# State-space stage of a decoder trunk: the rotated drive is added on TensorE, with new tables, tap layout and order

## Chip, cores and metric

The kernel runs on one core of one Trainium2 chip. The metric is the device time of an execution in microseconds; each measurement is the median of several executions. The profile is of one further execution.

## The reference, cut to what matters

A trunk of two layers on 512 tokens of 1024 channels, all in f32. The first layer is a diagonal state-space mixer with a gated output and a squared-ReLU MLP; then come shared keys and values, an attention layer with forget gates and a second MLP. The change lies in the state-space mixer alone:

```python
lam_bar = jnp.exp(lam * dt)                       # 64 groups x 64 complex states
b_bar = ((lam_bar - 1.0) / lam)[..., None] * b
bu = jnp.einsum('blgc,gpc->blgp', uf, b_bar)      # 16 channels of a group drive 64 states
_, states = lax.associative_scan(_ssm_binop, (a_elems, bu), axis=1)   # s[t] = lam_bar*s[t-1] + bu[t]
y = jnp.real(jnp.einsum('blgp,gcp->blgc', states, c))
y = y + d_skip.reshape(N_GROUPS, SSM_GROUP) * uf
z = jax.nn.gelu(y.reshape(bsz, length, D_MODEL))
zw = z @ w_glu
return zw[..., :D_MODEL] * jax.nn.sigmoid(zw[..., D_MODEL:])
```

## The kernel before

The 64 groups are worked in eight blocks `b` of 8 groups. The 512 tokens are cut into 64 chunks of T = 8. Real and imaginary parts of the 64 states fill the 128 partitions. Within a chunk the answer is a causal filter with eight taps of 16 x 16 (a Toeplitz matrix per group); between chunks the state runs through a scan. A step of the scan multiplies by a complex number; the kernel splits this into its size (r8, in the scan) and its angle, which is undone before the scan and put back behind it, by tables of cosine and sine per group and chunk. For one block these are the steps; the names are those of `ORDER`:

- `win1, win2, wina` build the input matrix Win: two DVE products of 1024 elements, and an accumulating transfer of POOL's queue that adds tB to Win (512 KB). `wo1, wo2, woa` do the same for the output matrix, the first half of the tile TW.
- `pw, wt`: eight TensorE transposes of Win and two ACT copies. `pd` (`c_pd`): the drive, eight matmuls from WinT and the transposed inputs Uall into a bank of PSUM.
- `tab0, tab3`: the tables CS. DVE adds a coarse and a fine angle, and six ACT passes (four absolute values, two sines, L368 to L373) make cosine and sine.
- `cos, ds, da`: the drive times cosine into cc, the drive times minus sine into dt, both on DVE, and two accumulating transfers that add dt to cc with the partition halves swapped (`add_swapped`, L345).
- `dec, scan`: the decays, and the scan over cc into tz (L647). `P1, P2, padd`: the states times cosine and sine, again two products and two swapped additions by transfer. `py2`: states times output matrix.
- `pt, ks, kd, kw, tr`: the taps. Eight matmuls with 16 columns of weights (the last step of Win), each of 128 columns of Wout, go to partitions r to r+16 of two banks; two ACT copies put them into `ks`, DVE adds the skip term at lag 0, one transfer of SP's queue writes them to a DRAM buffer (`KD`, two of them), and `tr`, also on SP's queue, reads them back as a Toeplitz matrix into the second half of TW. `py1` multiplies the inputs with it. py1 and py2 add up in one bank; each alternates between the left and the right 64 columns of the array.
- `gelu, zt, zh, lo`: GELU on ACT, four transposes, a rounded copy by ACT and the remainder by DVE, both written with a stride so that tokens come in order.
- `gl, gs, gv, gp`: the first weights of the gated output (GLU): load, rounding, remainder, and matmul pieces that need only the first four blocks of Z. GLU accumulators hold two banks of PSUM for each of the groups 0, 1 and 2.

The order of the stage is written out by hand: each word of `ORDER` issues the instructions of a step to their engines, which run them in that order, each waiting for its operands. Apart from that, buffers set waits. Win has three, tB and P two, TW four (two of each kind A and B, handed out by the string `WQ`), PSUM eight banks. Behind the stage comes the rest of GLU (L810), where TensorE is busy throughout.

## Time and profile before

| | us |
|---|---|
| median of 3 runs | 1204.86 (1197.44 to 1206.99) |
| profiled execution, its own time | 1199.35 |
| its span | 1197.6 |
| mean granted TensorE clock over the span | 0.972 |

The span is what the profiler saw from the first to the last instruction; the execution's own time holds 1.75 us more. In the rows, L12 is line 12 of the kernel, PE is TensorE's matmuls, DVE VectorE, ACT ScalarE, POOL GpSimd and SP the engine whose queue issues most transfers. `x32` counts instructions; an f32 matmul is two of them. An idle time stands in brackets with what ended it.

### The profile page before, as it was taken

Reading aid. Unit: us, or ns where it says so; the run is one execution under the profiler, and the core shown is the slowest. Engines: PE = TensorE matmul, PEld = TensorE weight load, DVE = VectorE, ACT = ScalarE, POOL = GpSimd, SP = SyncE. Lnnn points to the kernel's source line nnn. Section 1 sums busy time; section 2 is a strip of 40 time slices with the busy share of each in tenths; the row PEclk is TensorE's granted clock in tenths of the full one; section 3 lists DMA queues with packets and bytes.
Section 4 is the critical chain, followed back from the end, with each engine's and each line's share of the span. In section 5 each row is a group of like instructions: output and inputs, shape, how many; then the busy total and the mean of one; then the engine's idle time right before and its main releaser. Section 6 shows DMA issues by size and latency. Waiting matters only on the chain.

```text
span 1197.6 us, 19030 instructions
## 1 busy us (share of the span) xinstructions
PE 1119.2 (93%) x7189; PEld 996.8 (83%) x7189; DVE 912.1 (76%) x1639; ACT 607.8 (51%) x1106; POOL 291.2 (24%) x298
## 2 busy tenths in 40 slices
PE   1678899999999999999999999888899999999997
PEld 1567688899999898998888999776899898999986
DVE  8976548799877778768566878875999777778754
ACT  4985355454434444336345666554755444343433
POOL 4234214422121212203102222314322312213101
PEclk9878899999999999999999999989899999999999
DMA  7997753143322323233244444311143323233222
GB/s 165 218 183 151 176 165 106 42 143 99 122 90 90 107 86 124 88 103 117 65 132 133 107 107 133 98 54 53 35 128 104 111 82 124 88 117 96 89 88 71
DMA packets 109388, 131.37 MB, mean 110 GB/s; under 512 B 9360, under 2 KB 87984, under 8 KB 109296
## 3 DMA queue, kind: packets, MB, share of 16 engines
q1 hardware_dynamic: 104432, 117.57, 32.9%
q0 software_dynamic: 4864, 12.59, 6.1%
q8 instruction: 57, 0.93, 0.3%
q14 instruction: 35, 0.29, 0.1%
HBM read 103.21 MB, written 2.74 MB: 88 GB/s over the span
## 4 chain that ended last, share of the span: by engine, by line
PE 79%; DVE 8%; DMA 5%; ACT 3%; issue 3%; SPq 0%; POOL 0%; DVEq 0%; ACTq 0%; POOLq 0%
PE pu L919 25%; PE po L810 16%; PE pvs L1484 14%; PE pk L810 6%; PE pv L810 6%; PE pvs L1130 2%; PE po L1268 2%; DMA cc<-dt 1%; PE ptp L1234 1%; PE pf L1118 1%; DMA TW<-tB 1%; DVE prob L1229 1%; DMA bc<-in_ssm_b_im_dram 1%; DMA TW<-kd 1%; PE pv L731 1%
## 5 line engine op out<-in xcount | busy, mean ns | idle before, releaser
L919 PE MATMUL pu<-hm,ar 128*128 128x256 f32 x1536 | 228.9, 284 | 3.2 <-ACT hm L863 2.2
L919 PEld LDWEIGHTS pu<-hm,ar 128*128 128x128 f32 x1536 | 204.4, 193 | 4.5 <-ACT hm L863 2.6
L810 PE MATMUL po<-at,wt 128*128 128x512 f32 x768 | 176.9, 389 | 0.0
L1484 PE MATMUL pvs<-wt,at 128*128 128x512 f32 (+1 forms) x768 | 175.5, 388 | 0.0
L898 POOL TENSOR_TENSOR ar<-ar,st 128x256 f32<-128x256 f32 x62 | 71.8, 1160 | 423.1 <-DVE ar L894 404.3
L124 ACT ACTIVATE wt<-st 128x1024 fp32r<-128x1024 f32 x110 | 116.2, 1057 | 114.0 <-PE po L810 30.3
L810 PEld LDWEIGHTS po<-at,wt 128*128 128x128 f32 x768 | 143.2, 188 | 29.1
L1484 PEld LDWEIGHTS pvs<-wt,at 128*128 128x128 f32 x768 | 142.6, 188 | 28.8
L128 DVE TENSOR_TENSOR wt<-st,wt 128x1024 fp32r<-128x1024 f32 x90 | 117.1, 1302 | 27.9 <-ACT wt L124 27.7
L919 PE MATMUL pu<-hd,x 128*128 128x256 f32 x768 | 136.3, 285 | 0.0
L887 ACT ACTIVATE ar<-ar 128x512 fp32r<-128x512 f32 x128 | 77.0, 627 | 89.9 <-PE pu L919 83.7
L919 PEld LDWEIGHTS pu<-hd,x 128*128 128x128 f32 x768 | 113.4, 193 | 2.9 <-issue 0.5
L888 DVE TENSOR_TENSOR ar<-ar 128x512 fp32r<-128x512 f32 x128 | 88.8, 700 | 31.0 <-ACT ar L887 31.0
L887 ACT ACTIVATE x<-st 128x512 fp32r<-128x512 f32 x62 | 36.3, 625 | 99.8 <-PE pvs L1484 48.9
L128 POOL TENSOR_TENSOR wt<-st,wt 128x1024 fp32r<-128x1024 f32 x20 | 48.2, 2408 | 143.6 <-ACT wt L124 125.5
L894 DVE TENSOR_TENSOR ar<-st 128x512 f32<-128x512 f32 x62 | 50.6, 819 | 32.8 <-DMA st<-in_mlp_w_dram 32.1
L810 PE MATMUL pv<-zt,wt 128*128 128x512 f32 x312 | 72.4, 391 | 0.2 <-ACT hT L992 0.2
L810 PEld LDWEIGHTS pv<-zt,wt 128*128 128x128 f32 x312 | 58.2, 188 | 12.3 <-ACT hT L992 0.4
L1220 ACT ACTIVATE prob<-psx,mx 128x128 f32<-128x128 f32 (+1 forms) x64 | 33.8, 528 | 60.2 <-DVE mx L1218 60.2
L899 POOL TENSOR_TENSOR ar<-ar,st 128x256 f32<-128x256 f32 x62 | 60.4, 977 | 4.2
L1039 ACT ACTIVATE at<-c 128x512 fp32r<-128x512 f32 x64 | 39.7, 630 | 39.3 <-DVE c L1037 39.1
L1025 DVE TENSOR_TENSOR hT<-hT,po 128x512 f32<-128x512 f32 x64 | 43.4, 679 | 16.8 <-PE po L810 16.8
(333 smaller groups left out, 2046.2 us busy)
## 6 DMA issues: line engine op xcount, KB each, us to landing
st<-in_mlp_w_dram SPq DMA_DIRECT2D x126, 512.0 KB
st<-in_ssm_w_glu_dram SPq DMA_DIRECT2D x16, 512.0 KB
st<-in_w_kvf_dram SPq DMA_DIRECT2D x14, 512.0 KB
hx<-kt SPq DMA_DIRECT2D x48, 128.0 KB
Win<-tB POOLq DMA_DIRECT2D x8, 512.0 KB, 7.3
TW<-tB POOLq DMA_DIRECT2D x8, 512.0 KB, 6.3
TW<-kd SPq DMA_DIRECT2D x8, 512.0 KB
st<-in_attn_wq_dram SPq DMA_DIRECT2D x8, 512.0 KB
```

Of the source, the lines that this page charges most:

```text
L124: S.activation(wt[:, 0], st, AF.Copy)
L128: (G if slot[1] == "A" and CFG["x"][7 + lows[0] % 3] == "G" else V).tensor_tensor(wt[:, 1], st, wt[:, 0].bitcast(F32), op=ALU.subtract)
L810: TE.matmul(pts[m], wt[:, a, k, m * P:(m + 1) * P], acts[k0 + k][:, b], start=(first and k0 == parts[0][0] and k == 0 and n == 0), stop=(k ...
L887: S.activation(X[0], src, AF.Copy)
L888: V.tensor_tensor(X[1], src, X[0].bitcast(F32), op=ALU.subtract)
L894: V.tensor_tensor(Ta[:, :, js].rearrange("p w j n -> p j w n"), f[:, :, 1:3], f[:, :, 0:1].broadcast_to([P, 2, 2, P]), op=ALU.add)
L898: e.tensor_tensor(Tb[:, 0, js], Ta[:, 0, js], v[:, :, 1, 0], op=ALU.add)
L899: e.tensor_tensor(Tb[:, 1, js], Tb[:, 0, js], v[:, :, 1, 1], op=ALU.add)
L919: TE.matmul(self.acc[p], self.W[p][:, a, j], self.H.moving(p, j, b), start=(p == g[0] and j == 0 and n == 0), stop=(p == g[-1] and j == 3 ...
L1025: V.tensor_tensor(hT[:, m, :], hT[:, m, :], po[j], op=ALU.add)
L1039: S.activation(at_[:, 0], c, AF.Square)
L1484: TE.matmul(po[:, cols], A[k][:, b], wts[k // 2][:, a, k % 2, cols], start=start and n == 0, stop=stop and n == 3 * len(ks) - 1)
```

## The change

- The drive. One DVE instruction `(CS - 1) * drive` makes both rotated parts at once (`c_cd`, 1024 elements). `da` is now two TensorE matmuls into one bank, the first part times the identity, the second times a signed swap of the partition halves (`swp`); the scan reads that bank. The states get the same single instruction (`c_pp`); their addition `padd` stays a transfer.
- The tables. `tab0` makes two angles (the second shifted by a quarter turn, whose rounding is added to `tk` and `ta`), and `tab3` is a sine and a square with factor, 2 sin^2, which is one minus the cosine of the double angle.
- The taps. `pt` takes 32 columns of weights (the last two steps of Win, of which the last counts), goes round four column groups of the array, and fills a quarter of one bank per group; `ks` is one copy over 128 partitions; `kd` adds on 128 partitions; `kw` is four transfers per block with runs of 128 bytes; there are four DRAM buffers. The skip term's tile and mask are laid out accordingly (`dl`, `dg`), and the zeros of the DRAM buffers come from a small tile.
- The last transposes write their bank with a stride of four, so that `zh` and `lo` read and write contiguously.
- The gain of the first two blocks moves from POOL to DVE. Six memsets of constants go or change.
- `ORDER` and `WQ` are new. Among other things: blocks 0 and 1 are begun together, the rest of the group factors (`LR`, `mR`) stands behind their products, the transposes of the inputs (`u`) stand ahead of the first `pw`, tables 0 and 4 ahead of `wt_0`, and pieces of GLU groups 0 and 1 ahead of block 5.

```diff
@@ -33,25 +33,24 @@
-WQ = "AABBABABAB"
+WQ = "BAABBABBAB"
 ORDER = """
...
+tk dl_0 gR gl_0 rxv gnl decS_0 win2V_1 sw_2_0 xsS_0_0 sw_2_1 win2V_0 xsS_1_0 gl_1 win1V_0 gl_2 kz win1V_1
+wina_0 xsS_1_1 gn wo1V_0 wina_1 dl_1 xsS_0_1 wo2V_1 u_6 sw_0_1 u_3 wo1V_1 u_2 u_1 usS_2 taV woa_1 u_4 usS_1
+tab0V_0 u_0 usS_4 u_5 usS_0 tab0V_4 u_7 tab3_0 tab0V_1 tab3_4 wo2V_0 pw_0 tab0V_2 woa_0 wtS_0 LR tab3_2 pd_0
+mR usS_7 pw_1 usS_3 dg usS_5 win2V_2 wtS_1 win1V_2 gs_1 pd_1 win2V_3 usS_6 wina_2 tab3_1 wo2V_2 pt_1 wo1V_2
...
+py2_4 cd_7 pw_6 gelu_4 wo1V_7 zt_4 woa_7 wtS_6 da_7 tr_5 pd_6 scan_7 decS_6 pp_7 pt_6 cd_6 padd_7 zt_3 ksS_6
+kd_6 zhS_3 da_6 kw_6 lo_3 zhS_4 lo_4 pt_7 scan_6 gp_1_3 ksS_7 kd_7 kw_7 gp_0_3 gp_1_2 tr_6 py1_5 tr_7 py2_5
+gp_0_2 pp_6 gs_2 gelu_5 gv_2 padd_6 py1_6 gp_2_0 py1_7 py2_7 gp_2_1 gelu_7 py2_6 zt_5 gp_2_3 zhS_5 gelu_6 lo_5
...
@@ -193,6 +187,10 @@
             dup = sp.tile([P, 64], F32, name="dup")
             G.tensor_copy(dup[0:64], ident[0:64, 0:64])
             G.tensor_copy(dup[64:128], ident[64:128, 64:128])
+            swp = sp.tile([P, P], F32, name="swp")
+            G.memset(swp, 0.0)
+            G.tensor_scalar(swp[0:64, 64:128], ident[0:64, 0:64], -1.0, None, ALU.mult)
+            G.tensor_scalar(swp[64:128, 0:64], ident[64:128, 64:128], -1.0, None, ALU.mult)
             pa = pst("pa")
             for h in range(2):
...
@@ -243,16 +241,16 @@
             mask = sp.tile([P, GC], F32, name="mask")
             for q in range(4):
-                G.tensor_copy(mask[q * 32:q * 32 + 32], ident[q * 32:q * 32 + 32, q * 32:q * 32 + GC])
-            ks = sp.tile([P, T, GB, GC], F32, name="ks")
-            G.memset(ks, 0.0)
-            KD = [dp.tile([GC, 2 * T - 1, P], F32, name=f"kd{i}", tag=f"kd{i}", bufs=1) for i in range(2)]
+                G.tensor_copy(mask[q * 32:q * 32 + 32], ident[q * 32:q * 32 + 32, q * 32 + GC:q * 32 + 2 * GC])
+            zk = sp.tile([GC, P], F32, name="zk")
+            G.memset(zk, 0.0)
+            KD = [dp.tile([GC, 2 * T - 1, P], F32, name=f"kd{i}", tag=f"kd{i}", bufs=1) for i in range(4)]
             def dl(i):
-                for h in range(2):
-                    v = (ssm_d, mix_norm)[i][0][h * 512:h * 512 + 1]
-                    DMA.dma_start(dgb[i][:, h * GB:h * GB + GB].rearrange("p g c -> p (g c)"),
-                                  bass.AP(tensor=v.tensor, offset=v.offset, ap=[[P, 4], [0, 32], [1, P]]))
+                v = (ssm_d, mix_norm)[i][0][0:1]
+                for q in range(4):
+                    DMA.dma_start(dgb[i][q * 32:q * 32 + 32],
+                                  bass.AP(tensor=v.tensor, offset=v.offset + q * 32, ap=[[0, 32], [P, NB], [1, 32]]))
             def gnl():
                 for i, gsrc in enumerate((mlp_norm[0], kv_norm, mix_norm[1], mlp_norm[1])):
...
@@ -359,18 +357,15 @@
             def tab0(q, e=G):
                 gs = slice(q * GB, (q + 1) * GB)
                 CS[q] = ap_.tile([P, 2, GB, NCH], F32, name="cs", tag="act")
-                e.tensor_tensor(CS[q][:, 1].rearrange("p g (a b) -> p g a b", a=T),
-                                tA[1][:, gs, :].unsqueeze(3).broadcast_to([P, GB, T, T]),
-                                tA[0][:, gs, :].unsqueeze(2).broadcast_to([P, GB, T, T]), op=ALU.add)
+                for i in range(2):
+                    e.tensor_tensor(CS[q][:, i].rearrange("p g (a b) -> p g a b", a=T),
+                                    tA[1][:, gs, :].unsqueeze(3).broadcast_to([P, GB, T, T]),
+                                    tB_[:, i, gs, :].unsqueeze(2).broadcast_to([P, GB, T, T]), op=ALU.add)
             def tab3(q):
-                co, si = fl(CS[q][:, 0]), fl(CS[q][:, 1])
-                S.activation(co, si, AF.Abs)
-                S.activation(si, si, AF.Abs, bias=sg[:, 9:10])
-                S.activation(co, co, AF.Abs, bias=sg[:, 8:9])
-                S.activation(si, si, AF.Abs, bias=sg[:, 8:9])
-                S.activation(co, co, AF.Sin, scale=TWO_PI, bias=sg[:, 4:5])
-                S.activation(si, si, AF.Sin, scale=sg[:, 6:7], bias=sg[:, 7:8])
+                t = CS[q].rearrange("p i g j -> p (i g j)")
+                S.activation(t, t, AF.Sin, scale=3.1415925)
+                S.activation(t, t, AF.Square, scale=math.sqrt(2.0))
             ss = sp.tile([P, T], F32, name="ss")
             junk = bp.tile([P, 512], F32, name="junk", tag="P3", bufs=1)
...
@@ -453,6 +448,12 @@
                     V.tensor_scalar(tks[i], tA[i], MAGIC, MAGIC, ALU.add, ALU.subtract)
                     yield
                 V.tensor_tensor(tA[1], tA[1], tks[1], op=ALU.subtract)
+                yield
+                V.tensor_tensor(tA[0], tA[0], tks[0], op=ALU.subtract)
+                yield
+                V.tensor_scalar(tB_[:, 1], tA[0], sg[:, 7:8], None, ALU.add)
+                yield
+                V.tensor_scalar(tks[1], tB_[:, 1], MAGIC, MAGIC, ALU.add, ALU.subtract)
             GA, GR = slice(0, 2 * GB), slice(2 * GB, NG)
...
@@ -585,31 +586,32 @@
                     cpy(e, WT[b][:, hf * 4:hf * 4 + 4, :], PW[b][hf].rearrange("p (g c) -> p g c", g=4))
             def b_pt(b):
-                TP[b] = [pst("pt") for _ in range(2)]
-                r = b % 4 * 32
-                for g in range(GB):
-                    TE.matmul(TP[b][g // 4][r:r + GC, (g % 4) * P:(g % 4 + 1) * P], W["Win", b][:, g, T - 1],
-                              W["Wout", b][:, g], start=True, stop=True)
+                TP[b] = pst("pt")
+                for gh in range(2):
+                    for q in range(4):
+                        TE.matmul(TP[b][q * 32:q * 32 + 32, gh * P:(gh + 1) * P],
+                                  W["Win", b][:, 2 * q + gh, T - 2:T].rearrange("p t c -> p (t c)"),
+                                  W["Wout", b][:, 2 * q + gh], start=True, stop=True)
+
+            KS = {}
             def b_ks(b, e=S):
-                r = b % 4 * 32
-                for hf in range(2):
-                    cpy(e, ks[r:r + GC, :, hf * 4:hf * 4 + 4].rearrange("p l g c -> p g l c"),
-                        TP[b][hf][r:r + GC].rearrange("p (g l c) -> p g l c", g=4, c=GC))
+                KS[b] = bp.tile([P, T, 2, GC], F32, name="ks", tag="ks", bufs=2)
+                cpy(e, KS[b].rearrange("p l g c -> p g l c"),
+                    TP[b][:, 0:2 * P].rearrange("p (g l c) -> p g l c", g=2, c=GC))
             def b_kd(b):
-                r = b % 4 * 32
-                d = ks[r:r + GC, 0]
-                V.tensor_tensor(d, d, dgb[0][r:r + GC, b // 4 * GB:(b // 4 + 1) * GB], op=ALU.add)
+                d = KS[b][:, 0]
+                V.tensor_tensor(d, d, dgb[0][:, b].rearrange("p (g c) -> p g c", c=GC), op=ALU.add)
             def b_kw(b):
-                r = b % 4 * 32
-                DMA.dma_start(KD[b % 2][:, T - 1:2 * T - 1].rearrange("c l n -> c (l n)"),
-                              ks[r:r + GC].rearrange("p l g c -> p (l g c)"))
+                for q in range(4):
+                    DMA.dma_start(KD[b % 4][:, T - 1:2 * T - 1, q * 32:q * 32 + 32],
+                                  KS[b][q * 32 + GC:q * 32 + 2 * GC].rearrange("p l g c -> p l (g c)"))
             def b_tr(b):
                 Toep = W["TW", b][:, 1].rearrange("p g t c -> p (g t c)")
-                v = KD[b % 2][0:1, 0:1, 0:1]
+                v = KD[b % 4][0:1, 0:1, 0:1]
                 DMA.dma_start(Toep, bass.AP(tensor=v.tensor, offset=v.offset,
                                             ap=[[P, T], [(2 * T - 1) * P, GC], [1, T * P]]))
                 TP[b] = Toep.rearrange("p (t g c) -> p g t c", g=GB, c=GC)
...
@@ -628,34 +630,39 @@
                               start=True, stop=True)
                 DD[b] = PD[b].rearrange("p (g j) -> p g j", g=GB)
-            def c_cos(b):
-                CC[b] = g2("cc", 2)
-                V.tensor_tensor(CC[b], DD[b], CS[b][:, 0], op=ALU.mult)
-
-            def c_ds(b):
-                DS[b] = g2("dt")
-                V.scalar_tensor_tensor(fl(DS[b]), PD[b], -1.0, fl(CS[b][:, 1]), op0=ALU.mult, op1=ALU.mult)
+            def rot(o, b, v):
+                V.scalar_tensor_tensor(o, CS[b], 1.0, v.unsqueeze(1).broadcast_to([P, 2, GB, NCH]),
+                                       op0=ALU.subtract, op1=ALU.mult)
+
+            def c_cd(b):
+                CC[b] = bp.tile([P, 2, GB, NCH], F32, name="cc", tag="cc", bufs=1)
+                rot(CC[b], b, DD[b])
+
+            DA = {}
+
+            def turn(name, a):
+                pd = pst(name)
+                for i, m in enumerate((ident, swp)):
+                    TE.matmul(pd, m, fl(a[:, i]), start=i == 0, stop=i == 1)
+                return pd
             def c_da(b):
-                add_swapped(fl(CC[b]), fl(DS[b]))
+                DA[b] = turn("da", CC[b])
             TZ = {}
             def c_scan(b):
                 tz = bp.tile([P, GB * NCH + 1], F32, name="tz", tag="tz", bufs=1)
                 V.memset(tz[:, 0:1], 0.0)
-                V.tensor_tensor_scan(tz[:, 1:GB * NCH + 1], fl(CC[b]), fl(DEC[b]), 0.0, op0=ALU.add, op1=ALU.mult)
-                PP[b] = [g2("P1", 2), g2("P2", 2)]
+                V.tensor_tensor_scan(tz[:, 1:GB * NCH + 1], DA[b], fl(DEC[b]), 0.0, op0=ALU.add, op1=ALU.mult)
                 TZ[b] = tz[:, 0:GB * NCH].rearrange("p (g j) -> p g j", g=GB)
-            def c_p2(b, e=V):
-                e.tensor_tensor(PP[b][1], TZ[b], CS[b][:, 1], op=ALU.mult)
-
-            def c_p1(b, e=V):
-                e.tensor_tensor(PP[b][0], TZ[b], CS[b][:, 0], op=ALU.mult)
+            def c_pp(b):
+                PP[b] = bp.tile([P, 2, GB, NCH], F32, name="PP", tag="PP", bufs=2)
+                rot(PP[b], b, TZ[b])
             def c_padd(b):
-                add_swapped(fl(PP[b][0]), fl(PP[b][1]))
+                add_swapped(fl(PP[b][:, 0]), fl(PP[b][:, 1]))
             def py(b, w, u, start, stop):
                 for g in range(GB):
...
@@ -680,25 +687,21 @@
             def e_zt(b):
                 ZP[b] = pst("zt")
+                zv = ZP[b].rearrange("p (j h t) -> p h j t", h=2, t=4)
                 for t in range(4):
-                    TE.transpose(ZP[b][:, t * P:(t + 1) * P], YU[b][:, t].rearrange("p g c -> p (g c)"), ident)
-
-            def zview(b, i):
-                return Z[b][:, i].rearrange("p (j h t) -> p h t j", h=2, t=4)
-
-            def zsrc(b):
-                return ZP[b].rearrange("p (t h j) -> p h t j", h=2, t=4)
+                    TE.transpose(zv[:, :, :, t], YU[b][:, t].rearrange("p g c -> p (g c)"), ident)
             def e_zh(b, e=S):
                 Z.append(act_t("zt"))
-                cpy(e, zview(b, 0), zsrc(b))
+                cpy(e, Z[b][:, 0], ZP[b])
             def e_lo(b):
-                V.tensor_tensor(zview(b, 1), zsrc(b), zview(b, 0).bitcast(F32), op=ALU.subtract)
+                V.tensor_tensor(Z[b][:, 1], ZP[b], Z[b][:, 0].bitcast(F32), op=ALU.subtract)
             def dg():
                 V.tensor_tensor(dgb[0], dgb[0], dgb[1], op=ALU.mult)
-                V.tensor_tensor(dgb[0], dgb[0], mask.unsqueeze(1).broadcast_to([P, 2 * GB, GC]), op=ALU.mult)
+                d = dgb[0].rearrange("p b (g c) -> p (b g) c", c=GC)
+                V.tensor_tensor(d, d, mask.unsqueeze(1).broadcast_to([P, 2 * NB, GC]), op=ALU.mult)
             def gn():
                 pg = pst("pg")
```

## Rows read from the trace of the kernel before

**Rows 1.** The page's first line: span of the profiled execution
```profile
span 1197.6 us, 19030 instructions
```

**Rows 2.** Windows: PE, PEld, DVE, ACT, POOL busy, clock, DMA share, GB/s
```profile
40.00:60.00 20.00, 13.58 (x89) 11.69 (x85) 19.44 (x24) 19.26 (x33) 8.24 (x11) 0.80 1.01 204
60.00:80.00 20.00, 13.87 (x150) 11.71 (x148) 17.34 (x23) 17.61 (x28) 7.96 (x12) 0.84 1.03 189
80.00:100.00 20.00, 15.27 (x194) 14.18 (x194) 11.80 (x18) 17.08 (x29) 7.96 (x11) 0.76 0.85 169
100.00:120.00 20.00, 20.00 (x225) 17.50 (x224) 12.49 (x18) 8.81 (x13) 7.54 (x12) 0.83 0.75 144
120.00:140.00 20.00, 15.70 (x152) 12.90 (x151) 10.93 (x17) 7.74 (x10) 6.22 (x10) 0.85 0.82 167
```

**Rows 3.** TensorE's timeline: start, us, instructions, [idle before, releaser]
```profile
43.64 1.91 PE L591 MATMUL pt<-TW,Win 128*16 128x128 f32 x16 [1.17 <-DMA TW<-tB]
...
81.50 1.97 PE L663 MATMUL py<-TW,Uall 128*64 128x64 f32 x32 [5.43 <-ACT ks L353]
...
132.16 1.15 PE L663 MATMUL py<-TW,P 128*64 128x64 f32 x32 [1.94 <-DMA P<-P]
134.79 1.98 PE L663 MATMUL py<-TW,Uall 128*64 128x64 f32 x32 [1.48 <-DMA TW<-kd]
...
150.29 1.65 PE L731 MATMUL pv<-zt,wt 128*128 128x512 f32 x6
```

**Rows 4.** Chain of waits, first 230 us: start, us, what
```profile
49.05 5.83 DMA cc<-dt
...
75.69 10.97 DMA cc<-dt
```

**Rows 5.** Instructions by form, 40 to 160: busy, mean ns, idle before
```profile
L697 DVE TENSOR_TENSOR zt<-zt 128x512 fp32r<-128x512 f32 x8 | 9.2, 1146 | 7.8 <-ACT zt L353 7.6
L353 ACT ACTIVATE zt<-zt 128x512 fp32r<-128x512 f32 x8 | 9.0, 1131 | 13.1 <-PE zt L684 13.0
...
L353 ACT ACTIVATE ks<-pt 16x512 f32<-16x512 f32 x16 | 8.9, 581 | 7.2 <-PE pt L591 7.1
...
L531 DVE TENSOR_TENSOR Win<-ML,XY 128x1024 f32<-128x1024 f32 x7 | 8.5, 1217 | 3.7 <-PE pt L591 3.7
...
L373 ACT ACTIVATE cs<-cs,sg 128x512 f32<-128x512 f32 x8 | 6.4, 798 | 0.0
...
L637 DVE SCALAR_TENSOR_TENSOR dt<-pd,cs 128x512 f32<-128x512 f32 x8 | 5.5, 689 | 8.6 <-DMA cc<-dt 8.5
...
L368 ACT ACTIVATE cs<-cs 128x512 f32<-128x512 f32 x8 | 5.0, 627 | 0.0
```

**Rows 6.** TensorE's timeline, the f32 matmul pb of the last MLP
```profile
873.11 1.02 PE L975 MATMUL pb<-dg,ones 128*128 128x512 f32 x2
873.56 0.92 PE L919 MATMUL pu<-hd,x 128*128 128x256 f32 x3
```

**Rows 7.** DMA queues, 0 to 172, then 18 to 26: packets, MB, share
```profile
q0 software_dynamic: 4864, 12.59, 42.4%
...
DMA packets 1831, 0.65 MB, mean 82 GB/s; under 512 B 1638, under 2 KB 1798, under 8 KB 1831
...
q1 hardware_dynamic: 1831, 0.65, 45.9%
```

**Rows 8.** Timeline, 20 to 45 us, DVE and TensorE
```profile
21.43 1.01 DVE L467 TENSOR_TENSOR LL<-tmp 128x384 f32<-128x384 f32 x2
...
25.18 1.21 DVE L536 TENSOR_TENSOR tB<-ML,XY 128x1024 f32<-128x1024 f32 x1
...
40.47 2.00 PE L627 MATMUL pd<-Uall,WinT 128*128 128x64 f32 x16
```

**Rows 9.** SP's queue: tap copies (min/median/max), the TW load's wait
```profile
L607 SPq DMA_DIRECT2D kd<-ks x8: 302/308/330, 48.4 to 128.2; - x8
...
SPq L613 <- DMA kd<-ks: 27.5, 6, 7.4
```

More of the change, by code (lines that the diff above doesn't have):

```diff
@@ L283, in body @@
             f8, f64 = small("f8"), small("f64")
-            tA = [sp.tile([P, NG, T], F32, name=f"tA{i}") for i in range(2)]
-            tks = [bp.tile([P, NG, T], F32, name="tk", tag="P2", bufs=2) for i in range(2)]
+            tB_ = sp.tile([P, 2, NG, T], F32, name="tAB")
+            tA = [tB_[:, 0], sp.tile([P, NG, T], F32, name="tA1")]
+            tks = [bp.tile([P, 2, NG, T], F32, name="tk", tag="PP", bufs=2)[:, 0] for i in range(2)]
             def angles():
```

51 lines of the change are left out of this document (18 added, 33 removed).

## Prediction

> **What bounds the kernel now.** Read the split of the execution first: the profiled one is 1199.35 us, its span 1197.6 [rows 1], and the three timed runs have a median of 1204.86 (1197.44 to 1206.99). One per cent, 12 us, is about what a measurement of this kernel can tell from no change. Everything that the change touches lies in the first 160 us, the state-space stage; what follows is matmul after matmul, so a microsecond gained here should be a microsecond gained at the end.
>
> Then read the stage in pieces of 20 us [rows 2]. From 40 to 140 us TensorE is busy 78.4 us of 100, so idle for 21.6. The granted clock lies between 0.76 and 0.85, a mix of stretches at 1.2 and at 2.4 GHz; busy time times what is missing of the clock (13.58 x 0.20 and four more) gives 14.4 us lost to it. So 36 us of TensorE's time could at most come back. In the same rows three other columns are nearly full: DVE 19.4 and 17.3 of 20 up to 80 us, ACT 19.3, 17.6 and 17.1 up to 100 us, the DMA engines 1.01 and 1.03 up to 80 us and 0.75 to 0.85 later. No single engine bounds the stage: it is a relay with little slack in the front and a queue of TensorE work at the back.
>
> Third, what ended TensorE's pauses [rows 3]. There are nine in this stretch. Three end with ACT (5.43 us the longest) and make 9.8 us; three end with the accumulating transfers into Win and TW (1.17 the first), 5.1 us; two with the accumulating transfer P (1.94 the second), 5.2 us; one, 1.48, with the round trip of the taps through DRAM. The chain of waits names a fourth kind that makes no TensorE pause of its own but holds DVE: cc<-dt, 5.83 and 10.97 us for two additions of the rotated drive [rows 4].
>
> **The change part by part.** *Drive added by TensorE.* Gone per block: two DVE products (0.69 us each) [rows 5] and two accumulating POOL transfers of 128 KB, whose 16 issues leave POOL's queue to Win, TW and P. New: one DVE instruction of 1024 elements, which I price at the 1.22 us of a 1024-element product [rows 5], since at 512 elements this form (0.689) costs what a product does; and two f32 matmuls of 512 columns. One such matmul is two instructions, and in the one place where before has it the second starts 0.45 us after the first [rows 6]: 0.9 us, so 1.8 us per block and 14.4 us for eight at 2.4 GHz, twice that at 1.2. The scan then reads PSUM; no row of the stage prices that, and I take no difference, since the drive's product dt reads PSUM at the price of any other 512-element product (its bounds: nothing, and the 0.53 us by which 1.22 exceeds 0.69).
> The new wait is that of da on its DVE product, in TensorE's own queue. Behind da_1 and da_0 stand the transposes and drive of block 2, behind da_7 and da_6 the drive of block 6 and the taps of block 7. The producer takes 1.22 us once DVE comes to it, and DVE's order puts it right after work that TensorE needs anyway. I count no pause for it beyond those that I leave standing below; in the middle, a DVE that is late by two of its 1024-element products would cost 2.4 us for each such da.
> Banks of PSUM come out even, as the taps take one instead of two and the added drive one; but the pieces of GLU group 1 now start before block 5, so GLU holds four of eight banks from there, where before it held two. Its cover is that a block's banks turn over while GLU pieces run.
>
> *Taps in four column groups.* Before, eight matmuls per block with 16 columns of weights take 1.91 us [rows 3], 0.119 per instruction of 128 columns. After, the same eight go to four column strips of the array. The nearest row is py, which alternates between two strips: 32 instructions of 64 columns in 1.15 us, 0.036 each, where half of 0.119 would be 0.060: a factor of 1.7 for two strips. Twice that factor once more gives 0.119 / 2.8 = 0.042, 0.7 us per block; the ends are 1.91 (no overlap) and 0.48 (four at once). I take 0.6 to 0.7 and a saving of 1.25 x 8 = 10 us. The Trainium skill, TensorEngine Tiling (Array Packing), Theoretical Speedup, allows up to four times for 32 columns or fewer, which would make the saving 11.4; Key Properties in it says that changing the tiling mode drains the engine, which before pays as well, with its 16-column weights.
> TensorE's net is thus +4 us at full clock; at the stage's mean clock, 0.82, it is +5.
>
> *Tables by sine squared.* Six ACT passes of 512 elements per block, 0.63 to 0.80 us [rows 5], 4.3 in all, become two of 1024; twice a single pass bounds each between 1.25 and 1.6, and overlapped issue takes some off: 2.5 per block, 1.8 less. DVE makes both angles: one more product, +0.69. The new order puts tables between gelus three times, so two more table loads.
> *Last transposes interleaved.* The strided copy and its remainder (1.13 ACT, 1.15 DVE) [rows 5] become contiguous, 0.6 and 0.69: half a microsecond less on each. The transposes now write strided; no row prices that, and I take nothing (its bounds are minus nothing and 0.6 us per block, doubling them).
> *Taps' copy.* Two ACT copies of 0.58 [rows 5] become one over 128 partitions, about 0.5. Together ACT loses some 2.9 us per block, 23 in the stage, and DVE stays even (-0.15, +0.69, -0.46 and little else). So the three pauses that ACT ends should go: **+9.8**.
>
> *What the DMA engines get back and pay.* The software queue takes 42.4% of 172 us for 12.59 MB [rows 7]: 5.8 us of all 16 engines per MB. The 2.1 MB of the drive free 12 us. But the taps go to DRAM in pieces of 128 bytes: 512 per block, 4096 in all. The nearest row is the stretch with 1638 packets under 512 bytes of 1831: 45.9% of 8 us x 16 engines / 1831 = 32 ns each [rows 7], so 4096 x 32 / 16 = 8 us. The net is 4 us of relief, and the drive's six microseconds of landing leave the path. I let half of the 10.3 us of pauses at accumulating transfers go: **+5**.
> The Trainium skill, DMA: Bandwidth & Descriptors, Specifications, says that under 512 bytes the engine reads, modifies and writes. Were each small piece then twice as dear, an estimate by that page, the 8 would be 16 us and the relief a loss of 4; the mechanism is a rival below.
>
> *Clock.* One and the same product py stands at 1.98 us right behind two pauses and at 1.15 elsewhere [rows 3]: the two levels of the clock. Fewer pauses should leave fewer stretches at the lower one. I take half of 14.4: **+7**.
>
> *Order and queues.* On DVE the reduction of angles, the gains and the row norms now stand ahead of the first Win products. Before, the rest of the group factors took DVE from 21.43 to 25.18, then came win2 and win1 of block 0 [rows 8]; the norms followed. After, these 3.75 us are postponed, and ahead of the end of win1_0 come the norms (sixteen tiny instructions, some 2.4), the angles and gains (seven instructions of 512 elements or so, by 0.4 to 0.69 each an estimate of 3.9) and win2 of block 1 (1.14 as issued): 2.4 + 3.9 + 1.14 - 3.75 = 3.7 us later. A part is covered, since the transposes of U, which before followed pw_0, run in that time; the first drive product, pd_0 at 40.47 [rows 8], I put **2 us** later (between 0 and 3.7).
> SP issues four tap transfers per block where it issued one of 0.31 us [rows 9]; the TW load behind them on SP already waits 4.6 us each time (27.5 over 6). Three more issues at 0.31 to 0.6 add 0.9 to 1.8 us, and what is queued behind on SP, the TW load of the block and the next GLU weights, waits as long. With four DRAM buffers instead of two the copies no longer wait for the load before last. For the middle blocks other work hides it. For the last block it does not: after its taps come the copy, the scan ahead and kd (2), four issues (2), the landing (4.6), then issue and landing of TW (4 to 5, an estimate below the 5.83 us of an accumulating transfer [rows 4]), some 13 us. Queued on TensorE against it are four GLU pieces (1.65 each [rows 3]), and both products of block 5: 9 us. So **4 us** stay exposed, where before lost 1.48.
>
> Sum: 9.8 + 5 + 7 = 22 recovered; 5 + 2 + 4 = 11 paid. **11 us faster**: 1188.4 for an execution like the profiled one, which was 5.5 below the median, so 1194 (1204.86 - 11) for the median, with 1188 to 1200 for this case alone.
>
> **Rivals.** *The relay closes up*: the drive's detour of six microseconds was what kept later blocks from starting, and GLU pieces, ready earlier, fill what is left. Then all pauses but the 1.48 go and 12 of 14.4 us of clock; the costs shrink to 4 + 2 + 2. 32 - 8 = 24: 1181. For it speaks that cc stands in the chain with 10.97 us for one block; against it the full DVE up to 80 us.
> *DMA stays the bound*: the small packets eat the relief, and accumulating transfers end the same pauses. 9.8 + 4 of clock - 11 = 3: 1202. For it speaks a share of 1.01 to 1.03.
> *The strips do not overlap*: the taps stay at 1.91 and 10 / 0.82 = 12 us of the sum fall away: 1206. Against it speaks py.
> *SP becomes the bound, slower than before*: the TW load waits on SP for its four tap transfers, and the next block's stand behind it. At 2.4 of issue, 9 of landing and 0.6 for the load, eight blocks take 96 us. From 52, the first copy's 48.4 [rows 9] plus the late start, that is 148 for the last load, where before issued it about eight after 128.2. Twelve later, with the 2 us of the order, less what ACT gives back in the tail, 13 in all: 1218. It decides from a landing of about 8 us; at 4.6 it is harmless.
>
> **How the numbers follow.** Forecast 0.40, closed relay 0.28, DMA bound 0.14, strips 0.08, SP 0.10. Faster by over 1% means under 1192.8: the closed relay and the lower third of the forecast, 0.40. Slower by over 1% is most of the SP case and a little of the strips, 0.10. The rest, 0.50, is within 1%. The range leaves out the lowest of the closed relay and the SP case: 1179 to 1210.
>
> **What would show it.** ACT's share between 40 and 100 falls from nine tenths to about six; pt takes 0.6 to 0.7 us per block; da takes 1.8 us at full clock, 3.6 at half; pauses ended by ACT vanish; the last GLU piece of the stage ends some 11 us earlier. I am wrong if DMA waits take those pauses over, if the granted clock stays at 0.82, or if py1 of the last blocks waits over 4 us for TW.

## The result, and the profile after

The changed kernel takes 1214.67 us (median of 4, 1213.57 to 1221.75), the kernel before, measured beside it, 1204.69. The ratio is 1.010 with a 95% interval of 1.006 to 1.014: slower by 10 us, where 11 us faster was forecast. The profiled execution took 1215.23 us, 15.9 more than the one of before (1199.35). That one lies 5 us under its kernel's median, so differences between these two traces are larger than between the medians. The span, to set beside [rows 1]:

```profile
span 1213.5 us, 19061 instructions
```

Windows of the kernel after, 40 to 140 us, with the columns of [rows 2]:

```profile
40.00:60.00 20.00, 12.82 (x79) 11.11 (x78) 14.54 (x21) 12.19 (x18) 2.58 (x3) 0.77 0.59 114
60.00:80.00 20.00, 17.24 (x189) 12.49 (x189) 18.53 (x23) 6.55 (x10) 5.26 (x8) 0.89 0.85 161
80.00:100.00 20.00, 17.03 (x185) 12.47 (x181) 18.30 (x22) 13.40 (x19) 5.94 (x9) 1.00 0.77 157
100.00:120.00 20.00, 13.73 (x121) 11.30 (x118) 11.08 (x14) 8.80 (x13) 4.49 (x7) 0.74 0.81 161
120.00:140.00 20.00, 14.93 (x130) 13.06 (x131) 6.45 (x8) 2.98 (x6) 3.59 (x6) 0.66 0.58 119
```

The fourth column is ACT, the seventh the DMA engines' share. ACT was relieved as intended (32 us busy from 40 to 100, before 54), and so were the DMA engines, except from 100 to 120. The third is DVE: busy 11.1 and 6.5 us in the two stretches from 100 to 140, it has run dry, and so has TensorE. No engine is full there, so this is a wait. The groups by form, 40 to 175 us, show that the new operations cost about what was forecast:

```profile
L646 PE MATMUL da<-cc,ident 128*128 128x512 f32 x16 | 10.1, 721 | 4.3 <-DVE cc L634 3.3 <-DVE ks L605 1.0
L634 DVE SCALAR_TENSOR_TENSOR cc<-cs,pd 128x1024 f32<-128x1024 f32 x8 | 9.7, 1216 | 18.0 <-PE pd L629 16.6 <-PE da L646 1.4
...
L367 ACT ACTIVATE cs<-cs 128x1024 f32<-128x1024 f32 x7 | 7.4, 1059 | 9.0 <-DVE cs L361 8.8
...
L592 PE MATMUL pt<-TW,Win 128*32 128x128 f32 x128 | 5.8, 314 | 0.5 <-DMA TW<-tB 0.5
...
L351 ACT ACTIVATE ks<-pt 128x256 f32<-128x256 f32 x8 | 3.1, 382 | 8.2 <-PE pt L592 8.2
```

The waits are another matter. First TensorE's, 20 to 180 us, then DVE's, 30 to 175 (total, times, longest):

```profile
PE py L670 <- DMA TW<-kd: 19.0, 6, 5.8
PE pd L629 <- ACT WinT L351: 5.5, 2, 4.4
...
PE da L646 <- DVE cc L634: 3.3, 3, 1.7
```

```profile
DVE wt L127 <- ACT wt L123: 17.6, 4, 11.4
DVE cc L634 <- PE pd L629: 16.6, 3, 9.0
DVE tz L657 <- PE da L646: 7.1, 3, 3.8
DVE tB L537 <- DMA TW<-tB: 5.6, 1, 5.6
```

DVE's first row, the remainders of the weights of GLU, is no mark of the changed kernel: old_order, the fastest run below, has 17.4 us of it. The wait of py1 for its loaded taps, 1.48 us before [rows 3], is 19.0. That alone need not cost anything; what matters is what stands behind it. TensorE's timeline after:

```profile
106.42 1.97 PE L670 MATMUL py<-TW,Uall 128*64 128x64 f32 x32 [5.75 <-DMA TW<-kd]
108.33 3.68 PE L629 MATMUL pd<-Uall,WinT 128*128 128x64 f32 x16
...
125.08 1.98 PE L670 MATMUL py<-TW,Uall 128*64 128x64 f32 x32 [5.59 <-DMA TW<-kd]
126.98 3.68 PE L629 MATMUL pd<-Uall,WinT 128*128 128x64 f32 x16
```

Each of the two long pauses lies ahead of a py1 (blocks 3 and 4), and right behind that py1 stands pd, the drive of a later block (5 and 7), which needs no taps. The chain of waits, 84 to 175 us, goes through this place:

```profile
103.01 14.81 DMA kd<-ks
...
117.96 7.07 DMA TW<-kd
...
125.08 1.98 PE py L670 x32
127.05 3.61 PE pd L629 x16
...
135.32 2.27 PE da L646 x4
...
137.68 1.24 DVE tz L657
```

Block 4's taps go to DRAM (14.81 us) and back (7.07), py1 runs, then pd, both at the lower clock (1.98 and 3.68 us, where 1.15 and 2.00 stand elsewhere), and so on to the scan (tz) of block 7, which has nothing to do with block 4's taps. The last four of the eight scans on DVE show the loss:

```profile
100.27 1.22 DVE L657 TENSOR_TENSOR_SCAN tz<-da,dec 128x512 f32<-128x512 f32 x1
...
117.94 1.22 DVE L657 TENSOR_TENSOR_SCAN tz<-da,dec 128x512 f32<-128x512 f32 x1 [2.33 <-PE da L646]
...
137.68 1.23 DVE L657 TENSOR_TENSOR_SCAN tz<-da,dec 128x512 f32<-128x512 f32 x1 [3.83 <-PE da L646]
...
143.50 1.22 DVE L657 TENSOR_TENSOR_SCAN tz<-da,dec 128x512 f32<-128x512 f32 x1 [0.90 <-PE da L646]
```

### The profile page after: what moved, and what is told of

Read it like the earlier page. It is cut to its first block, busy times and chain, and to the rows that moved or that the text cites. A ratio compares the mean times of both kernels' runs of the same rounds, so it can differ in the third digit from the quotient of the medians.

```text
span 1213.5 us, 19061 instructions
## 1 busy us (share of the span) xinstructions
PE 1126.2 (93%) x7221; PEld 996.6 (82%) x7221; DVE 907.5 (75%) x1632; ACT 586.4 (48%) x1068; POOL 284.4 (23%) x282
## 4 chain that ended last, share of the span: by engine, by line
PE 75%; DVE 9%; DMA 7%; issue 2%; ACT 2%; POOL 1%; SPq 1%; DVEq 0%; ACTq 0%; POOLq 0%
PE pu L921 24%; PE po L812 15%; PE pvs L1486 13%; PE pk L812 6%; PE pv L812 6%; DMA TW<-kd 2%; PE pvs L1132 2%; DMA kd<-ks 2%; PE po L1270 2%; DMA TW<-tB 1%; PE ptp L1236 1%; PE pf L1120 1%; DVE prob L1231 1%; PE pw L812 1%; DMA st<-in_mlp_w_dram 1%
## 5 line engine op out<-in xcount | busy, mean ns | idle before, releaser
L900 POOL TENSOR_TENSOR ar<-ar,st 128x256 f32<-128x256 f32 x62 | 80.5, 1300 | 424.2 <-DVE ar L896 376.2
L901 POOL TENSOR_TENSOR ar<-ar,st 128x256 f32<-128x256 f32 x62 | 59.0, 954 | 4.2
L1041 ACT ACTIVATE at<-c 128x512 fp32r<-128x512 f32 x64 | 39.7, 630 | 40.4 <-DVE c L1039 40.4
```

Source lines behind the costliest of these rows:

```text
L900: e.tensor_tensor(Tb[:, 0, js], Ta[:, 0, js], v[:, :, 1, 0], op=ALU.add)
L901: e.tensor_tensor(Tb[:, 1, js], Tb[:, 0, js], v[:, :, 1, 1], op=ALU.add)
L1041: S.activation(at_[:, 0], c, AF.Square)
```

## The experiments

Each kernel was timed beside the kernel before; ratios are to that kernel, with 95% intervals. The runs were made in four groups (four, four, four and three rows of the table), in which the kernel before had medians of 1203.82, 1202.29, 1205.63 and 1202.82 us. So medians of different groups compare to some 3 us, and where it matters the ratio stands beside the median.

| run | what it is | median us | ratio |
|---|---|---|---|
| old_taps | after, taps as before | 1213.44 | 1.0068 (1.0028 to 1.0108) |
| mr_first | after, LR and mR ahead of wo2V_0 | 1211.63 | 1.0074 (1.0044 to 1.0104) |
| no_wait | after, taps loaded from a buffer of zeros | 1212.64 | 1.0072 (1.0041 to 1.0103) |
| kw_act | after, tap copies on ACT's queue | 1215.14 | 1.0086 (1.0051 to 1.0121) |
| old_order | after's operations, before's order | 1196.89 | 0.9946 (0.9914 to 0.9977) |
| new_order | before's operations, after's order | 1236.08 | 1.0251 (1.0189 to 1.0314) |
| four_tw_mr | after, four TW buffers, mR first | 1211.55 | 1.0046 (1.0013 to 1.0079) |
| old_order_taps | old_order, taps as before | 1203.00 | 0.9990 (0.9957 to 1.0024) |
| py_late | after, four py1 moved back | 1209.81 | 1.0037 (1.0009 to 1.0065) |
| py_late_tw | four_tw_mr, four py1 moved back | 1212.59 | 1.0044 (1.0011 to 1.0077) |
| taps_unread | after, py1 reads no loaded taps | 1203.12 | 0.9974 (0.9957 to 0.9992) |
| old_order_drive | old_order, drive added by transfers | 1205.16 | 0.9979 (0.9952 to 1.0006) |
| old_order_unread | old_order, py1 reads no loaded taps | 1196.03 | 0.9923 (0.9900 to 0.9947) |
| old_order_py_early | old_order, two py1 moved forward | 1214.60 | 1.0086 (1.0056 to 1.0117) |
| old_order_cd | old_order, cd_0 moved forward | 1197.88 | 0.9963 (0.9943 to 0.9984) |

**Four causes by name.** The first four runs each take one suspect out of the changed kernel: the taps' new layout, the wait in the front, the landing of the tap copies, the place of their issue. (old_taps also has ks, kd, kw, mask, dl and dg as before, and its junk tile shares a tag with tz to fit.)

```diff
# old_taps
-                TP[b] = pst("pt")
+                TP[b] = [pst("pt") for _ in range(2)]
...
# mr_first
-... wo2V_0 pw_0 tab0V_2 woa_0 wtS_0 LR tab3_2 pd_0 mR usS_7 ...
+... LR mR wo2V_0 pw_0 tab0V_2 woa_0 wtS_0 tab3_2 pd_0 usS_7 ...
# no_wait
-                v = KD[b % 4][0:1, 0:1, 0:1]
+                v = KDZ[0:1, 0:1, 0:1]
# kw_act
-                    DMA.dma_start(KD[b % 4][:, T - 1:2 * T - 1, q * 32:q * 32 + 32],
+                    S.dma_start(KD[b % 4][:, T - 1:2 * T - 1, q * 32:q * 32 + 32],
```

old_taps expected: 

> The changed kernel with the taps alone as they were before: 16 columns of weights, two banks and two copies per block, one transfer per block with runs of 4096 bytes; the four DRAM buffers, the new order and all else stay. Theory 1 (the taps' way to DRAM in four transfers with 128-byte runs holds SP's queue and lands late, so that py1 waits for TW on TensorE's queue, 19.0 us in six pauses): those pauses shrink to under 6 us and, with some 10 us more TensorE time for pt, the time is 1200 to 1208. Theory 2 (the new order's front, where DVE waits 5.6 us for a tB buffer and ACT for late tables): no change, 1212 to 1217. Theory 3 (the copies land late behind large transfers on SP's ring, whatever their runs): pauses stay above 14 us, 1212 to 1218.

mr_first expected: 

> The changed kernel with LR and mR put back ahead of wo2 of block 0, so that the tB buffer that m_rest still holds is free by then. Theory 2: the 5.6 us pause of DVE and the late tables behind it go, 1207 to 1210. Theories 1 and 3: the gain of the front is lost again at py1's wait for TW, 1212 to 1216.

no_wait expected: 

> The changed kernel, but the Toeplitz load reads a DRAM buffer of zeros that was filled once, so that it waits for no tap copy; the four copies per block are still issued. The taps' part of the output is left out. Theories 1 and 3: py1's pauses go almost wholly (under 4 us) and the time falls by 10 to 17 us, 1198 to 1205. Theory 2: 1212 to 1216.

kw_act expected: 

> The changed kernel with the four tap copies per block issued from ACT's queue instead of SP's; the Toeplitz load stays on SP. Theory 3 (they land late because they stand behind 512 KB loads on SP's ring): landing falls from up to 14.8 us to under 5, pauses under 8 us, 1203 to 1208. Theory 1 in its narrow form (the number of small runs sets the landing, and four issues a block): pauses stay above 12 us, 1211 to 1217; ACT pays some 2 us a block for issuing.

All four stay within 4 us of the changed kernel, inside its interval. In old_taps py1's waits for its taps halve, from 19.0 to 9.8 us, and the time does not follow; but pt costs its 1.91 us per block again there, an estimated 10 us of TensorE (1.25 in each of eight blocks), which may hide a gain. In mr_first the wait at tB went from 5.6 to 3.4 us, but TensorE's wait for tap loads grew from 19.0 to 23.6 us in its profile (of the slowest of nine executions, 1218.10): what the front gained was lost again behind it. In kw_act that wait is 14.5 us. In no_wait, where the load reads zeros that have long been there, py1 still waits 16.0 us:

```profile
PE py L673 <- DMA TW<-kdz: 16.0, 6, 5.0
```

The load is issued by SP behind the block's copies, which wait for kd, and it takes its own time to land. So none of the four, taken out alone, brings the time back: not the layout, not the wait in the front, not the copies' landing, not the queue that issues them. Two of them together were not taken out.

**Order or operations.** The operations of one kernel were put into the order (and `WQ`) of the other; a merged product stands where the later of its halves stood. In four_tw_mr the second GLU weight and its pieces go to the end of the order, so that its TW buffer serves the blocks. Theory 4 is that the new order costs the time by itself, rival A that the new operations do.

```diff
# old_order
-WQ = "BAABBABBAB"
+WQ = "AABBABABAB"
-... scan_4 zt_2 wtS_5 pp_4 py1_3 zhS_2 tr_4 win2V_6 padd_4 decS_5 pd_5 ...
+... pd_6 pp_3 gelu_2 zt_1 padd_3 py1_3 zhS_1 wo1V_6 decS_4 lo_1 pw_7 ...
# four_tw_mr, beside mr_first's move
-WQ = "BAABBABBAB"
+WQ = "BABABABABA"
-... usS_5 win2V_2 wtS_1 win1V_2 gs_1 pd_1 ...
+... gp_0_2 pp_6 gs_2 gs_1 gelu_5 gv_2 gv_1 padd_6 gp_1_0 py1_6 ...
```

old_order expected: 

> The changed operations, all of them, issued in the order of the kernel before and with its sequence of weight buffers (each merged multiplication stands where the later of its two halves stood). Theory 4 (the new order is what costs: py1 is issued where its taps cannot have landed, and the front waits for a slot of the temporaries): the waits for the tap load on TensorE fall from 19 us to under 6, and the time is at or under the kernel before: 1190 to 1205, ratio 0.99 to 1.00. Rival A (the new operations cost more than their unit prices say, through da in TensorE's queue): 1210 to 1220, ratio above 1.005, whatever the order.

new_order expected: 

> The operations of the kernel before, all of them, issued in the new order and with the new sequence of weight buffers (the two halves of each merged multiplication one after the other). Theory 4: the order alone makes it slower, 1212 to 1225, ratio above 1.006, with waits of py1 for the tap load of over 12 us. Rival A: the order is neutral, 1200 to 1208, ratio 0.997 to 1.003.

four_tw_mr expected: 

> The changed kernel with two moves in its order: the second GLU weight (gs_1, gv_1 and the four gp_1 pieces) goes to the end, as in the kernel before, so that four buffers instead of three serve the eight blocks' Wout and taps, and LR and mR come before wo2V_0. Theory 4 in its narrow form (the loop through three buffers): the tap load is issued earlier, its waits fall from 19 us to about 10, and the time falls by 5 to 10 us, to 1204 to 1210. Rival: the order of py1 on TensorE's queue sets the waits, not the buffers: within 3 us of the changed kernel, 1211 to 1217, with the GLU pieces that filled the middle now missing there and found at the end.

old_order_taps expected: 

> The order and the tap layout of the kernel before, with the new drive (cd, da on TensorE), the new tables and the interleaved last transposes. Theory 4: 1190 to 1203, ratio 0.985 to 1.00, since the DMA path of the taps is as before and ACT and the software queue have less to do. Rival A (da in TensorE's queue costs more than its columns): at or over 1206, ratio above 1.002.

This settles the first question. With all its new operations in the old order the kernel is faster than before; with no new operation in the new order it is slower by 2.5%. Rival A is out. But new_order does not show the changed kernel's loss: py1 waits 2.4 us for its taps there, where over 12 were expected. The loss stands in DVE's waits instead: the scan stands so close behind the drive that it waits for the addition by transfer in four of the eight blocks.

```profile
DVE tz L646 <- DMA cc<-dt: 33.3, 4, 12.1
```

four_tw_mr is 3 us under the changed kernel, with overlapping intervals: the number of TW buffers is not the main cause. Its py1 waits only 9.5 us for taps, half of the changed kernel's 19.0, so the sum of these waits does not tell the time either. old_order's windows and TensorE's waits:

```profile
40.00:60.00 20.00, 11.49 (x94) 8.15 (x92) 19.97 (x25) 10.75 (x15) 4.28 (x5) 0.74 0.95 198
60.00:80.00 20.00, 16.01 (x154) 11.33 (x154) 19.92 (x24) 13.55 (x18) 6.29 (x10) 0.83 0.96 177
80.00:100.00 20.00, 15.41 (x207) 12.01 (x206) 12.44 (x17) 11.78 (x18) 5.11 (x7) 1.00 0.77 144
100.00:120.00 20.00, 19.15 (x248) 14.72 (x245) 13.53 (x17) 6.31 (x12) 5.52 (x9) 1.00 0.83 151
120.00:140.00 20.00, 17.37 (x165) 13.38 (x164) 10.92 (x13) 6.55 (x10) 4.97 (x8) 0.91 0.68 130
```

```profile
PE pw L580 <- DMA Win<-tB: 10.0, 3, 7.6
PE da L645 <- DVE cc L633: 7.6, 4, 4.6
PE py L669 <- DMA TW<-kd: 6.0, 2, 3.4
PE pt L591 <- DVE cs L360: 3.0, 1, 3.0
```

From 100 to 120 us TensorE is busy 19.15 us at full clock, where the changed kernel had 13.73 at 0.74. DVE waits nowhere for pd. Its last four scans:

```profile
105.17 1.22 DVE L656 TENSOR_TENSOR_SCAN tz<-da,dec 128x512 f32<-128x512 f32 x1
...
117.03 1.22 DVE L656 TENSOR_TENSOR_SCAN tz<-da,dec 128x512 f32<-128x512 f32 x1
...
124.24 1.22 DVE L656 TENSOR_TENSOR_SCAN tz<-da,dec 128x512 f32<-128x512 f32 x1
...
127.00 1.23 DVE L656 TENSOR_TENSOR_SCAN tz<-da,dec 128x512 f32<-128x512 f32 x1 [0.16 <-PE da L645]
```

At the fifth scan the new order was 5 us ahead; from the fifth to the seventh it takes 37.4 us, the old order 19.1. So the front is not where it loses. The landing by itself is not the cause either: SP waits as long for tap copies in old_order as in the changed kernel, which the waits of SP's queue show, first after, then old_order. With that the rival "SP becomes the bound" falls as a mechanism, though its time (1218) was the nearest: old_order has the same four copies and about the same waits on SP, and is faster than the kernel before.

```profile
SPq L615 <- DMA kd<-ks: 30.4, 11, 12.7
```

```profile
SPq L614 <- DMA kd<-ks: 32.6, 12, 12.0
```

**py1's place.** Theory 5: py1 is issued ahead of its taps' arrival, and holds up the pd that is queued behind it. One run moves it back, one leaves its wait out, and one asks what the drive on TensorE is worth (it has two buffers for cc, for which junk and dgg share other tags). Rival B is that the front or the buffers set the length.

```diff
# py_late (and py_late_tw, on four_tw_mr): one of the four moves
-... pp_4 py1_3 zhS_2 tr_4 win2V_6 padd_4 decS_5 pd_5 lo_2 wo2V_7 wina_6 pw_7 cd_5 gp_0_1 tab0V_7 wtS_7 tab3_7 da_5 wo2V_6 py2_3 ...
+... pp_4 zhS_2 tr_4 win2V_6 padd_4 decS_5 pd_5 lo_2 wo2V_7 wina_6 pw_7 cd_5 gp_0_1 tab0V_7 wtS_7 tab3_7 da_5 py1_3 wo2V_6 py2_3 ...
# taps_unread
-                py(b, TP[b], Uall[:, b * GB:(b + 1) * GB], True, False)
+                py(b, W["Wout", b], Uall[:, b * GB:(b + 1) * GB], True, False)
# old_order_drive
-                DA[b] = turn("da", CC[b])
+                add_swapped(fl(CC[b][:, 0]), fl(CC[b][:, 1]))
+                DA[b] = fl(CC[b][:, 0])
```

py_late expected: 

> The changed kernel with only TensorE's queue changed: four products of the loaded taps move back behind work that does not need them (py1_1 behind pd_3, py1_2 behind pt_3, py1_3 behind da_5, py1_4 behind pd_7). Theory 5: py1 waits for its tap load at the head of the in-order queue and pd of a later block, which is ready, stands behind it, so VectorE waits for pd (16.6 us in 3 in the changed kernel) and the next block's taps start late. Then VectorE's waits for pd fall under 6 us and the time falls by 8 to 14 us, to 1200 to 1207, ratio 0.995 to 1.003. Rival B (the front, or the number of TW buffers, sets the stage's length): the waits move from py1 to other lines and the time stays 1211 to 1217.

py_late_tw expected: 

> The same four moves on top of the order with four TW buffers and with LR and mR first. Theory 5: 1194 to 1202, ratio 0.990 to 0.998, at or under the changed operations in the old order (0.9946). Rival B: not under 1205, as without the moves (1211.55).

taps_unread expected: 

> The changed kernel with py1 multiplying Wout in place of the loaded taps, so that it waits for no tap copy or load; copies and loads are still made (the taps' part of the output is left out). Theory 5: with the head of the queue never waiting, 1196 to 1205, VectorE's waits for pd under 6 us. Rival B: 1211 to 1217, other waits take the place.

old_order_drive expected: 

> The changed operations in the old order, with the rotated drive added by two accumulating POOL transfers as before instead of on TensorE (added with the other sign, so the output is not the reference's), and two buffers for the drive. If the pauses that the prediction counted at these transfers (10.3 us, half of it to come back) less TensorE's extra columns are the gain: slower than with the drive on TensorE (1196.89) by 3 to 8 us, 1200 to 1205. Rival: the drive's move is worth nothing, within 2 us of it, 1195 to 1199, and the gain lies in the tables, the taps and the transposes.

taps_unread comes to 1203.12, 11.5 us under the changed kernel (15 by the ratios): most of what separates it from old_order. DVE's wait for pd falls from 16.6 to 0.8 us, even in its profile, which is of the slowest of ten executions (1209.46). py_late gains less than expected, 5 us by medians and 8 by ratios, with intervals that overlap, though its wait for pd vanishes too: py1 still waits 6.9 us, the scan's wait for da stays (6.6, before the move 7.1), and the next block's Wout waits for a buffer that py holds.

```profile
DVE tz L656 <- PE da L645: 6.6, 4, 3.3
...
DVE TW L531 <- PE py L669: 3.7, 1, 3.7
```

py_late_tw, which should have been the best, missed: 1212.59, over its expected 1202. Its profile is of one of the two executions under 1206 (the other five take 1210 to 1214), and even there the last scan, at 129.59 us, is close to old_order's. In old_order_drive DVE waits 11.5 us for the two transfers, and py1's wait for its taps grows from 6.0 to 17.8 (in a profile of 1208.04, nearly the slowest of ten); its median is 8 us above old_order's, but the two stand beside different runs of the kernel before, and by the ratios the difference is 0.3%, with overlapping intervals: a gain of some 4 us is likely, not proved.

**Three controls in the old order.** Would any order gain if the taps were not waited for? Does py1's place alone make the old order slow? Does the pause of da_0 in old_order cost anything?

```diff
# old_order_unread: old_order with taps_unread's edit
# old_order_py_early
-... tab3_5 pt_4 tr_3 py2_1 win1V_7 wina_7 pw_6 cd_4 ksS_4 wo1V_5 da_4 ...
+... tab3_5 pt_4 tr_3 py1_3 py2_1 win1V_7 wina_7 pw_6 cd_4 ksS_4 wo1V_5 da_4 ...
-... cd_5 tr_4 scan_4 da_5 pd_7 ...
+... cd_5 tr_4 py1_4 scan_4 da_5 pd_7 ...
# old_order_cd
-... tab3_0 pt_0 wo2V_2 wina_1 gv_0 woa_2 win2V_3 ksS_0 tab3_2 cd_0 kd_0 da_0 ...
+... tab3_0 pt_0 cd_0 wo2V_2 wina_1 gv_0 woa_2 win2V_3 ksS_0 tab3_2 kd_0 da_0 ...
```

old_order_unread expected: 

> The changed operations in the old order, with py1 multiplying Wout in place of the loaded taps (copies and loads are still made; the taps' part of the output is left out). It is the control for taps_unread, which gained 1.1 to 1.3 per cent in the new order. Theory 5 (it is the new order that puts py1 ahead of its taps): in the old order TensorE waits only 6.0 us for tap loads, so this gains little, 1191 to 1197, ratio 0.990 to 0.995. Rival C (any order would gain as much once the taps are not waited for, and the order as such has no part in it): 1181 to 1186, ratio about 0.983.

old_order_py_early expected: 

> The changed operations in the old order, with two products of the loaded taps moved forward in TensorE's queue, as the new order has them: py1_3 right behind tr_3 (so ahead of pw_6 and da_4) and py1_4 right behind tr_4 (ahead of da_5 and pd_7). Theory 5: some 5 us of waiting at each, the next blocks' drive behind them, and the time rises by 5 to 10 us over 1196.89, to 1202 to 1207, ratio 0.999 to 1.004. Rival B: TensorE has slack there, within 2 us, 1195 to 1199.

old_order_cd expected: 

> The changed operations in the old order, with the first rotated drive (cd_0) moved forward on VectorE by four operations, to where its tables are ready (46.8 us), so that da_0 does not hold TensorE's queue for 4.6 us. If that pause is on the path: 2 to 4 us under 1196.89, 1193 to 1195. If the stage is bound elsewhere by then (the transfers of the software queue): 1195 to 1199.

The first gains 0.9 us (3 by the ratios, with intervals that overlap): in the old order the taps are not waited for in a way that costs much. Beside taps_unread it makes a table of two by two. With the taps read, the order costs 17.8 us (1214.67 against 1196.89); unread, 7.1 (1203.12 against 1196.03). So 11 us of the order's cost pass through the loaded taps (12 by the ratios, give or take 7 by their intervals), and some 6 to 7 do not, which no run takes apart.

The second puts as much loss into the old order by moving two words: 1214.60, 17.7 us above old_order, more than the 5 to 10 expected. It shows what such a place can cost, not the changed kernel's share, since both words stand right behind their tap load, closer than in the new order. Its two waits of py1 make 16.6 us, and DVE stands idle for most of them:

```profile
101.45 1.98 PE L669 MATMUL py<-TW,Uall 128*64 128x64 f32 x32 [6.92 <-DMA TW<-kd]
...
123.07 1.98 PE L669 MATMUL py<-TW,Uall 128*64 128x64 f32 x32 [9.68 <-DMA TW<-kd]
124.97 2.08 PE L645 MATMUL da<-cc,ident 128*128 128x512 f32 x2
```

```profile
104.96 1.23 DVE L531 TENSOR_TENSOR TW<-LL,XY 128x1024 f32<-128x1024 f32 x1 [8.01 <-PE py L669]
...
132.91 0.19 DVE L604 TENSOR_TENSOR ks<-ks,dgb 128x32 f32<-128x32 f32 x1 [15.76 <-ACT ks L350]
```

DVE stands for 8.01 and 15.76 us: the first time because its next Wout needs a TW buffer that a py2 right behind py1 still reads, the second because its kd waits for ks, ks for pt, and pt stands behind py1 on TensorE. The third control changes nothing (1197.88): the pause at da fell from 7.6 to 3.9 us, and the pauses at Win's transfer grew from 10.0 to 13.2.

old_order is the fastest version that still uses its taps: 0.9946 of the kernel before.

## Why the prediction was wrong

- **The step that failed** is in "Order and queues": "For the middle blocks other work hides it." I priced the round trip of the taps for the last block alone (4 us), and the new order in the front alone (2). In the middle the new order issues py1_3 and py1_4 ahead of pd_5 and pd_7, and the work that should hide the load stands behind it in the same queue; they wait 5.75 and 5.59 us for their taps. The order costs 1214.67 against 1196.89, some 15 to 18 us by medians and ratios. Of these, 11 to 12 pass through the loaded taps; where the rest arises is open. The prediction nowhere held each py1 against the arrival of its taps, although the order and a price for the trip were at hand.
- The price was low as well: a TW load was put at 4 to 5 us, issue and landing; the chain after has 7.07 to 11.64 for one, and that of old_order_py_early 7.25 and 9.14. The trace of before had the number, in the chain that the prediction read for the drive's transfers:

```profile
124.14 10.52 DMA TW<-kd
```

That the last two blocks still expose about the 4 us forecast (waits of 2.56 and 2.01) is luck: the last load takes 11.64 us, and more work stood against it than was counted.
- **The front** (2 us) came as forecast: pd_0 starts at 42.21, 1.7 us later than before. The first scan is 8 us later than in old_order (66.58 against 58.44), but at the second the new order is ahead (70.22 against 73.91). mr_first shows no gain that can be told apart.
- **The operations** were forecast at 13 to 17 us of gain without the order (22 recovered, 5 for TensorE's net, 4 for the tail's taps). old_order measures 5.4. By its one profile the clock came back as forecast (busy time times what is missing: 7.3 us lost instead of 14.4), and the pauses that ACT ended fell from 9.8 to 1.2 us. But new ones took their place: da for its product 7.6 us ("I count no pause for it" was wrong), py1 4.5 us more, pt 3.0; and Win's transfer still ends 10.0 us. So TensorE's idle time from 40 to 140 us fell from 21.6 to 20.6 us, by 1.0 where 14.8 (9.8 and 5) were to come back. Removing a named pause did not by itself shorten the stage, as old_order_cd shows.
- **Which part gains?** In the old order the tap layout is worth 6 us by medians (1203.00 without it). The two were run in one group, and their ten executions each lie apart (1193.96 to 1199.34, 1201.09 to 1206.83), though the intervals of the ratios overlap. I charged its tail 4 us and its small packets 8 of DMA time. The hardware queue does take 44.8% of the first 175 us with them and 40.4 without, 7.7 us of all 16 engines, but the kernel is not slower for it. That the Trainium skill, DMA: Bandwidth & Descriptors, Specifications, has a read-modify-write for such pieces is not seen in the time of any run here: the layout as a whole, with its cheaper pt, gains.
- **Right**: da 1.8 to 1.9 us at full clock, pt at 0.65 per block, cc at 1.22, ACT's share (0.54 of 40 to 100 us), the vanishing ACT pauses. Taken at no cost, and none seen: the scan's read from PSUM (1222 ns, before 1220) and the transposes written with a stride (0.66 us, as before). For pt, 1.91 to 0.65 is a factor of 2.9 for four column groups, under the fourfold that the Trainium skill, TensorEngine Tiling (Array Packing), Theoretical Speedup, allows.
- **The clock** in the changed kernel loses 13.5 us by the windows, about as before: the granted clock rose in the two stretches in which TensorE is busier than before (60 to 100) and fell in the other three. That it would stay near 0.82 was one of the prediction's own signs of being wrong, and so was that DMA waits take the pauses over; both came.
- **Open**: why moving the four py1 back regains only 5 of 11.5 us (8 of 15 by ratios), and why py_late_tw gains nothing on top. The waits that take their place are named above; none was removed alone. The traces add one thing. In py_late_tw the last scan is 2.6 us behind old_order's (129.59 against 127.00), but from 40 to 140 us TensorE has run 30 of GLU's matmul instructions, against 53 in old_order and 24 in the changed kernel. So in that execution the scans are back in time, and what is still lost is GLU work that TensorE has yet to do when they end.

## What to carry to other kernels

In a hand-written order, hold each consumer of a transfer against the transfer's arrival, in the middle of the pipeline as much as at its end, and look at what is queued behind it on the same engine: a wait at the head of an in-order queue can cost its full length when the next block's first step stands behind it (16.6 us of waits cost 17.7), and little elsewhere (6.0 us cost 1 to 3 in old_order). The sum of such waits does not say which; a run that takes the wait away, in both orders, does. When a change brings operations and an order together, run the new operations in the old order first; here that splits 10 us lost into 5 gained and 15 lost. Unit prices can all be right and the sum have the wrong sign.

## What the runs showed that was not expected

Two words of the order, two waits of together 16.6 us, cost 17.7 us: beside the head of TensorE's queue there was hardly any slack, though no engine is full in that stretch (TensorE 11.94 and 14.53, DVE 10.25 and 5.43 us busy of 20, by the windows of old_order_py_early from 100 to 140). The chain of waits of the changed kernel has pieces of 1.63 to 14.81 us for the landing of tap copies, 64 KB per block each time.
